# Expert rows by an indirect DMA from DRAM, and a scatter in two float32r passes

## The chip, the core and the metric

The kernel runs on one core of one Trainium2 chip. A core has a matrix engine (TensorE, PE, with its weight load PEld), VectorE (DVE), ScalarE (ACT), GpSimd (POOL) and SyncE (SP), and 16 DMA engines between DRAM and the on-chip memory. The metric is the device time of one execution in microseconds, as a median over runs.

## What is computed

Two transformer blocks over 512 tokens of 1024 features, in float32. The change lies in the last part of the first block, the expert choice: each of 16 experts takes the 64 tokens of highest affinity, applies its own gated network of three 1024 x 1024 matrices, and its results are added back to the rows of its tokens.

```python
def expert_choice_ffn(h, router_w, w_gate, w_up, w_down):
    cap = CAPACITY_FACTOR * n // N_EXPERTS                      # 64
    aff = jax.nn.softmax((h @ router_w).astype(jnp.float32), axis=-1)
    w_sel, idx = lax.top_k(aff.transpose(0, 2, 1), cap)
    xs = jax.vmap(lambda hb, ib: hb[ib])(h, idx)                # gather
    hid = jax.nn.silu(jnp.einsum('becd,edf->becf', xs, w_gate)) * jnp.einsum('becd,edf->becf', xs, w_up)
    ys = jnp.einsum('becf,efd->becd', hid, w_down) * w_sel[..., None]
    return ...zeros((n, d)).at[ib.reshape(-1)].add(yb.reshape(-1, d))   # scatter
```

Before it stand modulation, a gated linear recurrence, a convolution and an attention; after it the second block (pooling, delta rule, cross-attention with a memory, MLP).

## The kernel before

`build` (L1394 on) writes the program in stages. A scheduler orders each engine's instructions from the data dependences, the buffers of each tile and a priority by the order of the code, so the order of an engine need not be that of the source. Each engine works its list in order. Matrices of float32 are multiplied in two ways: as plain float32 (a matmul then shows as two records on PE), or split into a high and a low part of type float32r (`split`, L439: a cast on ACT, a subtraction on DVE), each product of parts being one record.

`route` (L796) computes the affinities `aff`, then the 64 largest of each expert by eight rounds of max and replace on DVE, and from them `slot`: for each token and expert its place among the 64, or a negative number. It also keeps `h2` (L834), the tokens times their 1/rms. While DVE does that, PE multiplies keys and values of the memory (`mem_kv`, eight units; L145 to L147 and L125 to L127); their results leave through `mst` (ACT) and a store on the GpSimd queue (`mk_dram`, `mv_dram`).

`expert_pair(p)` (L867) handles experts 2p and 2p+1 side by side, 64 rows each. `G` (L871) is a one-hot matrix of tokens by slots. `XT` is the pair's input, features by slots: 32 products of `h2` with `G` into PSUM (`xtp`, L880), then eight DVE operations with gain and shift (L883). Then come three products with the experts' matrices by `pair_mm` (L856): 32 matmuls each, alternating between the two halves of the PE columns, one half for each expert (L864, `pair`). After the gate product stand the sigmoid on ACT and DVE, `GT` (the transpose of `G`, through `gtp`) and `ws` (each slot's weight, through `wsp`, L899). After the up product the product of both is transposed (`htp`, L909) to `hT`, which shares its buffer with `XT` (L36, L907). After the down product DVE makes `ys`, the weighted rows (L915). `scatter` (L919) multiplies `GT` with `ys` for each tile of 128 tokens and half of the features (`sps`, L922, one plain float32 matmul), and DVE adds the result to the residual `x1` (L924). The program in front of the loop is short:

```python
        for p in range(8):
            last = self.expert_pair(p)
            if p == DL:
                self.delta_load()
            if p < 7:
                for t in range(4):
                    self.scatter(t, *last)
```

The last pair's scatter stands in `entry2` (L1006), which begins the second block. `delta_load` (L1034) brings constants of the second block on the GpSimd queue (`f2`, `maskf`, `baw`, `al`).

The weights come by `eload` (L845) on the SyncE queue: 24 loads of 1 MiB a pair, 192 in all. Two loads, one for each expert, serve eight matmuls, one step of `pair_mm`. They land in 18 buffers, nine for the even experts and nine for the odd ones, in fixed rotation; some are buffers that `mem_kv` used for its own weights. SyncE issues a load when PE has read its buffer for the last time. The first ten loads are issued ahead, beside the loads of the stages before.

Of the kernel before, what the change touches and what calls it, by code (L numbers as in the profile page):

```python
# [6 lines left out]
FT = mybir.dt.float32  # L7
FR = mybir.dt.float32r
U8 = mybir.dt.uint8
AF = mybir.ActivationFunctionType  # L10
# [4 lines left out]
D = 1024  # L15
KK = 8
S = 512
# [13 lines left out]
XB = 1  # L31
# [4 lines left out]
HT = lambda self: self.xtp  # L36
# [3 lines left out]
# columns of w_in  # L40
# [11 lines left out]
def shape_constants():  # L52
    i = np.arange(128)
    f = np.zeros((128, 466), np.float32)
# [11 lines left out]
    f[:, 450:466] = (np.float32(1.0) / np.arange(1, 17, dtype=np.float32))[None]  # L66
    f2 = np.zeros((128, 3, 128), np.float32)
# [11 lines left out]
class Net:  # L79
# [35 lines left out]
    def lin_f(self, *args, **kw):  # L115
        """ps[m, n] = W[:, c0:c0+m]^T X^T[:, t0:t0+n]"""
# [13 lines left out]
    def lin_f2(self, w, x, halves=False):  # L130
        """two tiles of lin_f; in halves of the tokens when the second half of x comes late"""
# [7 lines left out]
    def lin_n(self, ps, w, c0, x, t0, n, start=True, stop=True):  # L139
        """ps[128 tokens, n] = X[t0:t0+128] W[:, c0:c0+n]"""  # L140
# [11 lines left out]
    def rstd(self, ss, n, dst):  # L152
        """dst = (ss / n + eps) ** -0.5"""
# [4 lines left out]
    def log_sigmoid(self, dst, z, tmp):  # L158
        """dst = min(z, 0) - ln(1 + exp(-|z|)); tmp is overwritten"""
# [7 lines left out]
    def constants(self):  # L167
# [7 lines left out]
        self.kc = cp.tile([128, 466], FT, name="kc")  # L175
# [50 lines left out]
    def mod_cols(self, gs):  # L226
        """columns 256 g : 256 (g + 1) of the modulation, feature-major: four partial sums side by side, then their sum"""
# [18 lines left out]
    def pow_rstd(self, dst, ss, n, sub=None):  # L246
        """dst = (ss / n + eps) ** -0.5 for a few columns"""
# [4 lines left out]
    def norm_in(self):  # L252
        """self.hx: features by 512 latent tokens, self.hc: features by 256 context tokens, high and low parts"""
# [60 lines left out]
    def hgrn_head(self, hd, v):  # L314
        """both directions of a head. Index d: 0 forward, 1 backward, tokens in natural order, 256 context then 512 latent.
        F: products of the forget gates over blocks; Q[:, d]: keys times the gates from the key to the end of its block;
        R[:, 1 - d]: queries times the gates from the start of their block to the query. With blocks of m tokens, the pairs
        in neighbouring blocks of m come from the forward keys of the even blocks with the forward queries of the odd ones,
        and from the backward keys of the odd blocks with the backward queries of the even ones: one product for both."""
# [29 lines left out]
        # forget gate sigmoid(z), key sigmoid(-z)  # L349
# [9 lines left out]
        # products inside a chunk, transposed: the diagonal, then one level per block size  # L359
# [9 lines left out]
        def zigzag(x, n, m):  # L369
            """[n / 2m blocks, 2 halves, m]: the first row of x in the even blocks of m, its second row in the odd ones"""  # L370
# [3 lines left out]
        for lv in range(7):  # L374
# [10 lines left out]
            # blocks of twice the size  # L385
# [9 lines left out]
        # states: chunks 0, 1 are the context, 2 to 5 the latents  # L395
# [26 lines left out]
        # read-out: norm over the head, silu gate  # L422
# [27 lines left out]
    def gates(self, gate):  # L450
        """sigmoid(h W_gate)^T, a few products at a time, between those of others; self.sig holds it"""
# [13 lines left out]
    def merge(self, gate, wproj, first):  # L465
        """y^T (+)= sigmoid(h W_gate)^T * (o W_proj)^T, o in self.br"""
# [86 lines left out]
    def qk_stats(self, ps):  # L553
        """1 / rms of 2 token tiles of 4 heads of 64"""
# [8 lines left out]
    def qk_norm(self, dst, ps, stats, which, t):  # L563
        """dst[128, 2, 256] = 2 token tiles of 4 heads, normed, times the gain, rotated from tile t on"""
# [30 lines left out]
    def attn_keys(self, g):  # L595
        """[kh; kh] and [kl; kl] of a group of heads, 128 rows by 768 keys"""
# [993 lines left out]
```

## Time and profile before

| | us |
|---|---|
| device time, median of 3 runs (2608.29 to 2609.91) | 2608.99 |
| span of the profiled execution | 2604.0 |
| PE busy in it | 2528.8 (97%) |
| DVE, ACT busy | 1214.8, 982.5 |
| SyncE's queue, share of the 16 DMA engines over the span | 39.9% |

The profiled execution's own device time is not listed apart from its span; the runs are 5.0 us longer than the span. The rows further down are of five kinds. Windows give busy time, granted PE clock (1.00 is 2.4 GHz) and DMA rate of a stretch. The chain of waits follows what ended last backwards through the program and prints it in order of time, each piece with its start and length. The timeline lists instructions with the idle time ahead of them and what ended it. Groups by line give the busy time and the mean of one. DMA answers give the time from issue to landing. The expert stage runs from 1273 to 1790 us.

### The profile page before, as it was taken

To read this page: it belongs to the slowest core of one execution; us is meant where nothing else is said; L and a number is where in the kernel's file an instruction comes from. 1 tells how busy PE (TensorE), PEld (TensorE's weight loads), DVE (VectorE), ACT (ScalarE), POOL (GpSimd) and SP (SyncE) were. 2 spreads that over 40 slices of the span, in tenths; PEclk is the share of its full clock that TensorE was granted. 3 is DMA by queue.
4 is the path that set the end of the run, shared out by engine and by line. 5 is a ranking of instruction groups with operands and counts; after the bars stand their busy time and mean duration, and the time that the engine had idled before them with its cause. 6 is when DMAs were issued, how large, how long until landed. Compare 5 with 4: busy or idle time off the path is not lost.

```text
span 2604.0 us, 35253 instructions
## 1 busy us (share of the span) xinstructions
PE 2528.8 (97%) x14796; PEld 1927.7 (74%) x14796; DVE 1214.8 (47%) x1934; ACT 982.5 (38%) x1649; POOL 91.7 (4%) x116
## 2 busy tenths in 40 slices
PE   6999999999999999999999999998998999999998
PEld 4888888689887976679744444444778988889898
DVE  4558575734443565544422222124884464532433
ACT  4445445532234466633301000003665443431332
POOL 0000000000001110120100000000000010000000
PEclk9999999999999999999999999999999999999999
DMA  8223222422223210054899999994330032223331
GB/s 272 65 81 98 81 66 65 146 97 81 89 90 97 81 65 1 1 193 157 305 409 409 407 363 363 361 361 136 81 97 17 22 109 65 90 81 98 97 98 49
DMA packets 242494, 380.60 MB, mean 146 GB/s; under 512 B 6672, under 2 KB 188944, under 8 KB 242336
## 3 DMA queue, kind: packets, MB, share of 16 engines
q1 hardware_dynamic: 238784, 365.98, 39.9%
q0 software_dynamic: 3552, 12.38, 1.5%
q8 instruction: 116, 1.90, 0.3%
q14 instruction: 42, 0.34, 0.0%
HBM read 372.04 MB, written 4.19 MB: 144 GB/s over the span
## 4 chain that ended last, share of the span: by engine, by line
PE 80%; issue 12%; DVE 3%; ACT 3%; DMA 1%; POOL 0%; SPq 0%; POOLq 0%; ACTq 0%; DVEq 0%
PE pair L864 15%; PE lin L125 10%; PE lin L126 10%; PE lin L127 10%; PE lin L145 6%; PE lin L147 5%; PE lin L146 5%; PE xtp L880 2%; PE oT L717 2%; PE sps L922 2%; PE lps L383 2%; PE s L690 2%; PE ptp L704 1%; PE ups L408 1%; PE lin L234 1%
## 5 line engine op out<-in xcount | busy, mean ns | idle before, releaser
L112 DVE TENSOR_TENSOR wl<-raw,wh 128x1024 fp32r<-128x1024 f32 (+1 forms) x262 | 312.2, 1227 | 213.8 <-ACT wh L111 210.7
L111 ACT CAST wh<-raw 128x1024 fp32r<-128x1024 f32 (+1 forms) x262 | 258.4, 1028 | 400.1 <-PE lin L126 249.5
L864 PE MATMUL pair<-ew,XT 128*64 128x512 f32 x1024 | 239.4, 595 | 0.0
L127 PE MATMUL lin<-hx,wl 128*128 128x512 f32 x576 | 231.4, 402 | 0.0
L125 PE MATMUL lin<-hx,wh 128*128 128x512 f32 x576 | 229.8, 399 | 0.0
L126 PE MATMUL lin<-hx,wh 128*128 128x512 f32 x576 | 227.9, 396 | 0.0
L864 PEld LDWEIGHTS pair<-ew,XT 128*64 128x64 f32 x1024 | 81.9, 136 | 145.8 <-issue 139.9
L145 PE MATMUL lin<-wh,mh 128*128 128x256 f32 x512 | 145.0, 283 | 0.0
L147 PE MATMUL lin<-wh,ml 128*128 128x256 f32 x512 | 144.7, 283 | 0.0
L146 PE MATMUL lin<-wl,mh 128*128 128x256 f32 x512 | 144.0, 281 | 0.0
L864 PE MATMUL pair<-ew,hT 128*64 128x512 f32 x512 | 142.7, 599 | 0.0
L125 PE MATMUL lin<-hxh,wh 128*128 128x512 f32 (+1 forms) x352 | 131.6, 376 | 1.4 <-ACT hxh L941 1.3
L126 PE MATMUL lin<-hxl,wh 128*128 128x512 f32 (+1 forms) x352 | 131.8, 375 | 0.1
L127 PE MATMUL lin<-hxh,wl 128*128 128x512 f32 (+1 forms) x352 | 131.4, 374 | 0.0
L127 PEld LDWEIGHTS lin<-hx,wl 128*128 128x128 f32 x576 | 108.3, 188 | 25.7 <-issue 1.0
L125 PEld LDWEIGHTS lin<-hx,wh 128*128 128x128 f32 x576 | 108.4, 188 | 24.6 <-issue 1.2
L126 PEld LDWEIGHTS lin<-hx,wh 128*128 128x128 f32 x576 | 108.3, 188 | 24.7 <-issue 0.2
L864 PEld LDWEIGHTS pair<-ew,hT 128*64 128x64 f32 x512 | 44.7, 136 | 73.1 <-issue 68.7
L146 PEld LDWEIGHTS lin<-wl,mh 128*128 128x128 f32 x512 | 96.8, 189 | 0.1
L145 PEld LDWEIGHTS lin<-wh,mh 128*128 128x128 f32 x512 | 96.6, 189 | 0.1
L147 PEld LDWEIGHTS lin<-wh,ml 128*128 128x128 f32 x512 | 96.3, 188 | 0.0
L915 DVE SCALAR_TENSOR_TENSOR ys<-pair,ws,gfrow 128x512 f32<-128x512 f32 x16 | 12.0, 750 | 173.2 <-PE pair L864 172.3
(539 smaller groups left out, 5586.1 us busy)
## 6 DMA issues: line engine op xcount, KB each, us to landing
ew<-in_w_gate SPq DMA_DIRECT2D x64, 1024.0 KB, 14.1
ew<-in_w_up SPq DMA_DIRECT2D x64, 1024.0 KB, 14.2
ew<-in_w_down SPq DMA_DIRECT2D x64, 1024.0 KB, 8.7
raw<-in_w_in SPq DMA_DIRECT2D x34, 1024.0 KB, 5.1
raw<-in_w_in SPq DMA_DIRECT2D x52, 512.0 KB, 5.4
raw<-in_ada_w SPq DMA_DIRECT2D x24, 1024.0 KB, 6.3
raw<-in_w_up SPq DMA_DIRECT2D x16, 1024.0 KB, 5.6
raw<-in_w_down SPq DMA_DIRECT2D x16, 1024.0 KB, 5.2
```

The costliest lines, as they stand in the source:

```text
L111: nc.scalar.copy(wh[:, a:a + 4, :n], raw[:, a:a + 4, :n])
L112: nc.vector.tensor_sub(wl[:, a:a + 4, :n], raw[:, a:a + 4, :n], wh[:, a:a + 4, :n].bitcast(FT))
L125: self.nc.tensor.matmul(ps, a, xa, start=k == 0, stop=False)
L126: self.nc.tensor.matmul(ps, a, xb, start=False, stop=False)
L127: self.nc.tensor.matmul(ps, b, xa, start=False, stop=k == KK - 1)
L145: self.nc.tensor.matmul(ps, xa, a, start=start and k == 0, stop=False)
L146: self.nc.tensor.matmul(ps, xa, b, start=False, stop=False)
L147: self.nc.tensor.matmul(ps, xb, a, start=False, stop=stop and k == KK - 1)
L383: nc.tensor.matmul(ps[:, c].rearrange("p (b h x) -> p b h x", h=2, x=m), Xc[:, c], Y[:, c * n4:(c + 1) * n4], start=True, stop=True)
L690: nc.tensor.matmul(s[:, a:b], qT[2 * pair + hh][:, 128 * t:128 * t + 128], kT[p][:, a:b], start=p == 0, stop=p == 1)
L717: self.nc.tensor.matmul(self.oT[64 * hh:64 * hh + 64], self.vn[:, kt, 64 * g:64 * g + 64], PT[kt // 2][:, 2 * (kt % 2) + hh], start=kt == ...
L864: self.nc.tensor.matmul(ps[j][64 * e:64 * e + 64], lhs[:, k0 + k, 64 * e:64 * e + 64], w[e][:, k, 512 * j:512 * j + 512], start=k0 + k == ...
```

## The change

The normed tokens `h2` are no longer kept on chip: `route` writes them to a DRAM tensor `h2_dram` in four stores on the ScalarE queue, through two buffers. A table `affx` holds, for each token, the two affinities of a pair and the token's number (a new column of the constants). `expert_prep(p)` builds `G`, multiplies it with `affx` (`wsp`, three columns), casts the third column to an integer index `idx`, and starts an indirect DMA on GpSimd that brings the 128 token rows to `XG` (slots by features, one buffer). `expert_rows` transposes `XG` by eight PE transposes (`xtp`) and applies gain and shift as before. Pair 0 is prepared ahead of the loop; pair p+1 is prepared in `expert_pair(p)`, the gather written ahead of the up product, the transposes ahead of the down product. `hT` has its own buffer. `GT` becomes float32r, `ys` is split into high and low parts, and each scatter product is two float32r matmuls. Comments are also taken out, and line numbers shift.

```diff
@@ route
+        self.h2d = nc.dram_tensor("h2_dram", (S, D), FT, kind="Internal").ap()
+        for t in range(4):
+            h2 = rp.tile([128, D], FT, name="h2", bufs=2)
+            nc.scalar.activation(h2, x1[:, t], AF.Copy, scale=r[:, t:t + 1])
+            nc.scalar.dma_start(self.h2d[128 * t:128 * t + 128], h2)
...
-        self.h2 = sp.tile([128, 4, D], FT, name="h2")
-        for t in range(4):
-            nc.scalar.activation(self.h2[:, t], x1[:, t], AF.Copy, scale=r[:, t:t + 1])
+        self.affx = sp.tile([128, 4, 8, 3], FT, name="affx")
+        nc.vector.tensor_copy(self.affx[:, :, :, 0:2], aff.rearrange("p t (q e) -> p t q e", e=2))
+        nc.vector.tensor_copy(self.affx[:, :, :, 2:3], self.kc[:, 466:470, None, None].to_broadcast([128, 4, 8, 1]))
@@ expert_prep, expert_rows (new), expert_pair
-        XT = self.xtp.tile([128, KK, 128], FT, name="XT", bufs=XB)
+        ps = self.pp.tile([128, 3], FT, name="wsp", tag="tp", bufs=2)
+        for t in range(4):
+            nc.tensor.matmul(ps, Gf[:, t], self.affx[:, t, p], start=t == 0, stop=t == 3)
+        idx = self.sp.tile([128, 1], U32, name="idx", bufs=2)
+        nc.vector.tensor_copy(idx, ps[:, 2:3])
...
+        XG = self.xtp.tile([128, D], FT, name="XG", bufs=1)
+        nc.gpsimd.indirect_dma_start(out=XG, out_offset=None, in_=self.h2d,
+                                     in_offset=bass.IndirectOffsetOnAxis(ap=idx, axis=0), bounds_check=S - 1)
+        return Gf, ws, XG
...
+        XT = self.xtp.tile([128, KK, 128], FT, name="XT", bufs=1)
...
-                for t in range(4):
-                    nc.tensor.matmul(ps[:, j], self.h2[:, t, 128 * k:128 * k + 128], Gf[:, t], start=t == 0, stop=t == 3)
+                nc.tensor.transpose(ps[:, j], XG[:, 128 * k:128 * k + 128], self.ident)
...
-        GT = sp.tile([128, S], FT, name="GT", bufs=1)
+        GT = sp.tile([128, S], FR, name="GT", bufs=1)
...
+        if p < 7:
+            nGf, nws, XG = self.expert_prep(p + 1)
         u2 = self.pair_mm("w_up", p, XT)
-        hT = HT(self).tile([128, KK, 128], FT, name="hT", tag="XT", bufs=1)
+        hT = self.xtp.tile([128, KK, 128], FT, name="hT", bufs=1)
...
+        if p < 7:
+            self.pair = nGf, nws, self.expert_rows(XG)
         y2 = self.pair_mm("w_down", p, hT)
...
+            h, l = [sp.tile([128, 512], FR, name=f"ys{q}", bufs=2) for q in "hl"]
+            self.split(h, l, ys)
...
@@ scatter
-            self.nc.tensor.matmul(o, GT[:, 128 * t:128 * t + 128], ys2[j], start=True, stop=True)
+            for q in range(2):
+                self.nc.tensor.matmul(o, GT[:, 128 * t:128 * t + 128], ys2[j][q], start=q == 0, stop=q == 1)
@@ build
+        Gf, ws, XG = self.expert_prep(0)
+        self.pair = Gf, ws, self.expert_rows(XG)
         for p in range(8):
```

The scheduler's order on PE at the start of the stage, before (the last product of `mem_kv`, then pair 0):

```order
L147 MATMUL lin<-wh,mT_9130 128x256
L880 MATMUL xtp<-G,h_10124 128x128 x32
L864 MATMUL pair<-ew,XT 64x512 x32
L894 MATMUL gtp<-kc,G 128x128 x4
L899 MATMUL wsp<-aff,G 128x2 x4
L864 MATMUL pair<-ew,XT 64x512 x32
```

and after:

```order
L147 MATMUL lin<-wh,mT_9130 128x256
L884 MATMUL wsp<-affx,G 128x3 x4
L903 MATMUL xtp<-kc,XG 128x128 x8
L871 MATMUL pair<-ew,XT 64x512 x32
L923 MATMUL gtp<-kc,G 128x128 x4
L884 MATMUL wsp<-affx,G 128x3 x4
```

The 32 products ahead of the first gate product are gone; four short matmuls, the gather and eight transposes stand there.

On PE in the later pairs before, from the end of an up product to the scatter of the same pair (`hT` marks the down product, `XT` the next pair's gate):

```order
L909 MATMUL htp<-kc,sg 128x128 x8
L880 MATMUL xtp<-G,h_10124 128x128
L864 MATMUL pair<-ew,hT 64x512 x2
L880 MATMUL xtp<-G,h_10124 128x128 x6
L864 MATMUL pair<-ew,hT 64x512 x6
...
L864 MATMUL pair<-ew,hT 64x512 x14
L922 MATMUL sps<-ys,GT 128x512 x2
L864 MATMUL pair<-ew,XT 64x512
L922 MATMUL sps<-ys,GT 128x512 x2
```

and after:

```order
L934 MATMUL htp<-kc,sg 128x128 x8
L903 MATMUL xtp<-kc,XG 128x128 x4
L871 MATMUL pair<-ew,hT 64x512
...
L884 MATMUL wsp<-affx,G 128x3 x4
L871 MATMUL pair<-ew,hT 64x512 x24
L953 MATMUL sps<-ysh,GT 128x512
L871 MATMUL pair<-ew,XT 64x512
L953 MATMUL sps<-ysl,GT 128x512
L953 MATMUL sps<-ysh,GT 128x512
```

The one-hot products among the down product's matmuls are gone, and the `wsp` for the pair after the next stands there, so in the later pairs a gather is issued about a whole pair ahead of its transposes. The scatter still lies among the first matmuls of the next gate.

On GpSimd at the start of the stage before, with the waits of each instruction:

```order
L1001 DMA mv_dram<-mst 256x1x256 [waits DMASW7_49,Activation_49]
L1037 DMA f_11015<-in_kc 128x384 [waits DMASW5_49,DMASW6_49,DMASW4_49,DMASW7_49,DMASW2_49,DMASW0_49]
L209 DMA maskf<-in_km 128x448 [waits DMASW1_49,PE_49]
L1041 DMA baw<-in_w_in 128x8x8
L1043 DMA al<-in_ad 4x2 [waits DMASW3_49]
```

and after:

```order
L1032 DMA mv_dram<-mst 256x1x256 [waits DMASW7_49,Activation_49]
L1068 DMA f_11047<-in_kc 128x384 [waits DMASW5_49,DMASW6_49,DMASW4_49,DMASW7_49,DMASW2_49,DMASW0_49]
L891 DMA XG<-h_dram,idx 128x1024 [waits DMAHW4_49,DMAHW1_49,DMAHW5_49,DMASW1_49,DMAHW7_49,DVE_49,Pool_49]
L209 DMA maskf<-in_km 128x448 [waits PE_49]
L1072 DMA baw<-in_w_in 128x8x8 [waits DMASW3_49]
```

The first gather stands behind the load of `f2`, which waits for the landing of the stores ahead of it (`DMASW` are the semaphores of this queue's DMAs). The order of the weight loads on SyncE stays, but for two of the first up loads, which come behind a load of `mem_kv` instead of ahead of it.

## Rows read from the trace of the kernel before

**Rows 1.** Windows: busy us of PE, PEld, DVE, ACT, POOL; PEclk; DMA share; GB/s.

```profile
1290.00:1520.00 230.00, 228.79 (x1082) 100.41 (x1080) 49.04 (x90) 25.55 (x44) 0.56 (x1) 1.00 1.02 408
1530.00:1790.00 260.00, 258.86 (x1099) 107.86 (x1098) 53.82 (x104) 27.05 (x47) 0.00 (x0) 1.00 0.84 327
```

**Rows 2.** Chain of waits in an early pair: start us, us, what (x records).

```profile
1325.33 7.43 PE sps L922 x16
1332.76 6.92 PE xtp L880 x62
1339.68 13.88 PE pair L864 x64
...
1369.73 0.63 PE htp L909 x4
...
1384.66 7.43 PE sps L922 x16
```

**Rows 3.** Chain of waits in a late pair and at the stage's end.

```profile
1429.96 1.86 PE pair L864 x4
...
1433.36 3.58 PE pair L864 x12
...
1459.58 1.00 PE pair L864 x2
...
1476.72 20.76 PE pair L864 x92
...
1499.21 1.86 PE pair L864 x4
...
1775.98 13.95 PE pair L864 x64
...
1791.00 4.62 DMA fgrow<-in_rows
```

**Rows 4.** Timeline of PE in a projection with float32r parts.

```profile
302.47 0.39 PE L126 MATMUL lin<-hx,wh 128*128 128x512 f32 x1
302.70 0.39 PE L127 MATMUL lin<-hx,wl 128*128 128x512 f32 x1
```

**Rows 5.** Groups by line in 1270 to 1810: busy us, mean ns, idle before.

```profile
L924 DVE TENSOR_TENSOR x<-x,sps 128x512 f32<-128x512 f32 x64 | 43.5, 684 | 23.4 <-PE sps L922 23.2
...
L910 ACT COPY hT<-htp 128x512 f32<-128x512 f32 x16 | 9.4, 586 | 83.6 <-PE htp L909 83.6
```

**Rows 6.** SyncE's timeline at the start of the stage; landing of loads L853, 1100 to 1300.

```profile
1273.66 0.99 SPq L853 DMA_DIRECT2D ew<-in_w_down  x2
...
1283.96 0.88 SPq L853 DMA_DIRECT2D ew<-in_w_down  x2
...
DMA to landing us min/median/max: 4.9/8.4/15.9
```

**Rows 7.** Chain of waits at the start of the stage.

```profile
1273.21 7.14 PE xtp L880 x64
1280.35 13.88 PE pair L864 x64
```

**Rows 8.** GpSimd's timeline; DMA answers (KB, us to landing); weight loads issued 1270 to 1300.

```profile
1274.17 0.68 POOL L1001 DMA_DIRECT2D mv_dram<-mst  x1 [5.14 <-ACT mst L999]
1281.69 0.57 POOL L1037 DMA_DIRECT2D f<-in_kc  x1 [6.85 <-DMA mv_dram<-mst]
...
fgrow<-in_rows POOLq DMA_DIRECT2D x1, 512.0 KB, 4.6
...
mem<-in_mem POOLq DMA_DIRECT2D x1, 1024.0 KB, 10.5
...
DMA to landing us min/median/max: 5.7/11.4/15.9
```

**Rows 9.** Windows with PE partly idle, columns as in the first group.

```profile
20.00:30.00 10.00, 8.47 (x63) 2.91 (x56) 2.44 (x13) 1.18 (x4) 0.00 (x0) 1.00 1.04 333
1260.00:1265.00 5.00, 3.15 (x23) 2.93 (x22) 4.93 (x8) 0.52 (x2) 0.67 (x1) 0.85 0.72 251
```

More of the change, by code (lines that the diff above doesn't have):

```diff
@@ L9 @@
 U8 = mybir.dt.uint8
+U32 = mybir.dt.uint32
 AF = mybir.ActivationFunctionType
@@ L30 @@
 SOL = ((0, 8, 5, 1), (2, 9, 7, 3), (4, 6, 10, 11))
-XB = 1
 RB = 1
@@ L53, in shape_constants @@
     i = np.arange(128)
-    f = np.zeros((128, 466), np.float32)
+    f = np.zeros((128, 470), np.float32)
     f[:, :128] = np.eye(128)
@@ L66, in shape_constants @@
     f[:, 450:466] = (np.float32(1.0) / np.arange(1, 17, dtype=np.float32))[None]
+    f[:, 466:470] = i[:, None] + 128 * np.arange(4)[None]
     f2 = np.zeros((128, 3, 128), np.float32)
@@ L174, in constants @@
         nc.gpsimd.dma_start(self.pa, I["cols_a"])
-        self.kc = cp.tile([128, 466], FT, name="kc")
+        self.kc = cp.tile([128, 470], FT, name="kc")
         nc.gpsimd.dma_start(self.kc, I["kc"])
@@ L866, in pair_mm, with expert_prep @@
         return ps
-    def expert_pair(self, p):
-        nc, I, sp = self.nc, self.I, self.sp
+    def expert_prep(self, p):
+        nc = self.nc
         G = self.G[:, p % 2]
@@ L873, in expert_pair, with expert_rows @@
         Gf = G.rearrange("p t e s -> p t (e s)")
-        XT = self.xtp.tile([128, KK, 128], FT, name="XT", bufs=XB)
+        ps = self.pp.tile([128, 3], FT, name="wsp", tag="tp", bufs=2)
[3 more added lines that the diff above has]
+        nc.vector.tensor_copy(idx, ps[:, 2:3])
+        ws = self.sp.tile([128, 1], FT, name="ws", bufs=2)
+        for e in range(2):
+            nc.vector.tensor_copy(ws[64 * e:64 * e + 64], ps[64 * e:64 * e + 64, e:e + 1])
+        XG = self.xtp.tile([128, D], FT, name="XG", bufs=1)
+        nc.gpsimd.indirect_dma_start(out=XG, out_offset=None, in_=self.h2d,
+                                     in_offset=bass.IndirectOffsetOnAxis(ap=idx, axis=0), bounds_check=S - 1)
+        return Gf, ws, XG
+    def expert_rows(self, XG):
+        nc = self.nc
+        XT = self.xtp.tile([128, KK, 128], FT, name="XT", bufs=1)
         for a in range(2):
@@ L884, in expert_pair @@
                                         op0=OP.mult, op1=OP.add)
+        return XT
+    def expert_pair(self, p):
+        nc, I, sp = self.nc, self.I, self.sp
+        Gf, ws, XT = self.pair
         g2 = self.pair_mm("w_gate", p, XT)
@@ L894, in expert_pair @@
             nc.tensor.transpose(ps[:, 128 * t:128 * t + 128], Gf[:, t], self.ident)
-        GT = sp.tile([128, S], FT, name="GT", bufs=1)
+        GT = sp.tile([128, S], FR, name="GT", bufs=1)
         nc.scalar.copy(GT, ps)
-        ps = self.pp.tile([128, 2], FT, name="wsp", tag="tp", bufs=2)
-        for t in range(4):
-            nc.tensor.matmul(ps, Gf[:, t], self.aff[:, t, 2 * p:2 * p + 2], start=t == 0, stop=t == 3)
-        ws = sp.tile([128, 1], FT, name="ws", bufs=2)
-        for e in range(2):
-            nc.vector.tensor_copy(ws[64 * e:64 * e + 64], ps[64 * e:64 * e + 64, e:e + 1])
+        if p < 7:
+            nGf, nws, XG = self.expert_prep(p + 1)
         u2 = self.pair_mm("w_up", p, XT)
-        hT = HT(self).tile([128, KK, 128], FT, name="hT", tag="XT", bufs=1)
+        hT = self.xtp.tile([128, KK, 128], FT, name="hT", bufs=1)
         for j in range(2):
@@ L910, in expert_pair @@
             nc.scalar.copy(hT[:, 4 * j:4 * j + 4], ps)
+        if p < 7:
+            self.pair = nGf, nws, self.expert_rows(XG)
         y2 = self.pair_mm("w_down", p, hT)
-        ys2 = []
+        out = []
         for j in range(2):
@@ L915, in expert_pair @@
             nc.vector.scalar_tensor_tensor(ys, y2[j], ws, self.gfrow[:, 512 * j:512 * j + 512], op0=OP.mult, op1=OP.mult)
-            ys2.append(ys)
-        return GT, ys2
+            h, l = [sp.tile([128, 512], FR, name=f"ys{q}", bufs=2) for q in "hl"]
+            self.split(h, l, ys)
+            out.append((h, l))
+        return GT, out
     def scatter(self, t, GT, ys2):
```

1 line of the change is left out of this document (removed).

## The prediction

> **What bounds the kernel now.** The change touches the expert stage, so I looked for where that stage runs and which resource is short in it. The windows show it from 1273 to 1790 us with PE busy throughout, but with two different halves [rows 1]: in 1290 to 1520 the transfers run at 408 GB/s with the queues full (share 1.02), in 1530 to 1790 at 327 GB/s. So the weights press on the stage almost as hard as PE. A pair of experts needs 24 loads of 1 MiB, 25.17 MB, which at 0.408 MB/us take 61.7 us, or 2.57 us a load.
>
> The chain of waits gives PE's price for a pair. An early pair runs from one scatter to the next, 1325.33 to 1384.66: 59.3 us, less than the transfers need, so it eats from what was loaded ahead [rows 2]. A late pair, 1429.96 to 1499.21, takes 69.25 us, more than the transfers need [rows 3]: there PE is the bound, and SyncE waits for buffers. The reader should compare the pieces. Three products of 32 uninterrupted matmuls are 3 x 13.9 = 41.7 us in the early pair. In the late pair the scheduler has put the one-hot products and the scatter between them; its eleven runs of `pair` sum to 50.5 us (first 1.86 us for 4 records, last 20.76 us for 92). Two matmuls on the two column halves no longer run side by side at a run's end: 12 records alone take 3.58 us, where 12 x 0.217 = 2.6 would do. That is 8.8 us a pair for interruptions.
>
> **What the change removes on PE, per late pair.** (a) 32 one-hot products, 64 records, become 8 transposes. The records cost 6.92 us for 62 in one piece [rows 2] and 7.9 us plus two more records in pieces, 8.1 us in all; four transposes cost 0.63 us [rows 2], so eight 1.3. Gain 6.8 us. (b) The scatter: 8 fp32 matmuls cost 7.43 us [rows 2]. Two float32r passes are 16 matmuls of 128x512; the float32r projections follow each other at 0.23 us [rows 4], so 3.7 us. Gain 3.7 us. (c) Interruptions: the order of the changed kernel has runs of 1, 1, 6, 24, 1, 1, 3, 2 and 57 matmuls. By the rows of before, a run costs 0.43 us a matmul plus 0.57 where their number is odd (1.00 us for one) and 1.0 where it is even (1.86 for two, 20.76 for 46) [rows 3]: 41.3 + 6.4 = 47.7 instead of 50.5. Gain 2.8 us. (d) What it adds: the first scatter matmul now waits for the split of `ys` as well, a 0.6 us cast on ScalarE and a 0.7 us subtraction on VectorE (the sizes of the `hT` copy and of `x<-x,sps` addition) [rows 5]. Behind it on PE stand the next pair's gate matmuls, which have nothing to wait for but are in order. Between 0.6 (the subtraction hidden by the one gate matmul in between) and 2.6 (both halves in a row) us; I take 1.7. Net: 69.25 - 6.8 - 3.7 - 2.8 + 1.7 = **57.6 us** of PE per pair, in place of 59 to 69.
>
> **So the transfers become the bound.** 57.6 is less than 61.7. The gathers add to it: 128 rows of 4 KB, 0.52 MB, 1.3 us a pair by the same rate, 63.0 in all. From here I count the stage by the loads. There are 18 buffers for the loads. SyncE had issued the 18th by 1274.65, and the 19th only at 1283.96 [rows 6], when PE had finished the first step of the first gate: that product began at 1280.35 [rows 7], a step of 8 matmuls is 13.88 / 4 = 3.47 us, 1283.8. So the 19th load goes out 3.6 us after the gate product of pair 0 begins, and 174 loads remain. Everything depends on when that product begins.
>
> **The start, which gets worse.** Before, 32 one-hot products on PE (7.14 us) fill the time from 1273.2 to 1280.35 [rows 7]. After, PE sends the four `wsp` matmuls and then waits for the gather, which stands on GpSimd behind the load of `f2`. That load waits for the last `mv_dram` store: issued at 1274.17, and `f2` starts at 1281.69 after 6.85 us idle [rows 8]. The gather is therefore issued at about 1282.3. A delay on ScalarE comes ahead of it: `h2` is scaled through two buffers, so the third waits for a store, and the casts of the weights of `mem_kv` behind it wait too. Between 0 and 3 us of that reach PE (two scalings of 1.1 us and a store against one buffer of slack); I take 1.3, which moves the `mv_dram` store as well. The landing is not in the trace of before, since no indirect DMA is. The nearest rows are a 512 KB load on the same queue, 4.6 us, and a 1 MB one, 10.5 us [rows 8]; generating 128 addresses on GpSimd may cost more than a plain issue, so I take 6, with 4.6 and 10.5 as ends. The Trainium skill, "DMA: Bandwidth & Descriptors", section "Anatomy of one DMA", fits a GpSimd DMA by 2.0 us plus its bytes at 436 GB/s, an estimate of 3.2 us here; no run here shows that, the 4.6 us row is longer, and by the page the forecast would be 3 us lower. With 1282.3 + 1.3 + 6 = 1289.6, and 1.2 for four transposes and the first `XT` piece, the gate begins at **1291** (1288 to 1297) instead of 1280.35.
>
> PE then has been idle for some 16 us. After it had stood still for 1.85 of the 5 us from 1260 to 1265, the clock was granted at 0.85 on average there, so at 1.2 GHz for part of them [rows 9]. I let half of the first step run at 1.2 GHz: 3.47 + 1.7. The 19th load is issued at 1291 + 5.2 + 0.2 = 1296.5, 12.5 us later than before.
>
> **The sum.** 174 loads of 1.0486 MB and 7 gathers of 0.52 MB are 186.1 MB, at 0.408 MB/us 456 us. A lone load takes 4.9 us to land against 2.57 in the stream [rows 6], so 2.3 us on top: the last load lands at 1296.5 + 456 + 2.3 = 1754.8. The step on it is 3.5 us: PE ends the last product at **1758.3**, in place of 1775.98 + 13.95 = 1789.9 [rows 3]. PE by itself would be done at 1291 + 2 + 48 (pair 0, no scatter ahead) + 7 x 57.6 - 2 = 1742, so it has 16 us to spare, and every microsecond of (a) to (d) up to 2.3 a pair is hidden by the loads. At the end VectorE gets two more subtractions (1.4 us) ahead of the eight additions that it is busy with there, half hidden by the 4.62 us load of `fgrow` [rows 3]: +1. Gain 31.6 - 1 = 30.6 us. The profiled execution's span is 2604.0, 5.0 below the median of 2608.99, which I carry along: 2608.99 - 30.6 = **2578**. About 0.2% (5 us) is what a measurement of this kernel can tell from no change.
>
> **The rivals.** *The clock falls in the starved stretches* (7%). After the first pairs PE waits at each step, 3.47 us of work per 5.2 us of loads. For it: the dip above. Against: in 20 to 30 us PE was busy 8.47 of 10 us and stayed at full clock [rows 9]; and a step at 1.2 GHz takes 6.9 us, longer than its loads, so PE stops waiting. It can fall behind by one or two dips, 3 to 7 us, at the end: 2581 to 2585. In its extreme form (1%) each of the 96 steps runs at 1.2 GHz: 96 x 3.47 = 333 us on top of PE's own 1742, so some 2895, slower than before. The Trainium skill, "TensorE: Matmul & The Clock Gate", section "HAM oscillation", tells of a kernel that fell back to the low clock in every tile because it waited for its loads longer than it worked on them. The row of 20 to 30 us does not show that for waits like these.
>
> *PE stays the bound* (12%). If the scatter's waits or the interruptions are worse and a pair takes 62 us: 1291 + 50 + 7 x 62 - 2 = 1773, gain 16: 2593. For it: the scatter's additions on VectorE (0.68 us each for eight) pace PE through two PSUM buffers [rows 5].
>
> *The gathers come late: slower than before* (8%). `XG` has one buffer; the next gather is issued only when PE has read the last, and PE stands still at the transposes until it lands. With up to 18 weight loads outstanding, 46 us of transfers, a gather served after them would make pairs of gather plus some 5 us. From pair 0's start at 1291, the stage is slower than before from (1789 - 1341) / 7 = 64 us a pair, so from 59 us a gather; at 70 us: 1341 + 7 x 75 = 1866, 2685. For it: landings on that queue were measured with few loads outstanding. Against: the `mv_dram` store was done 7.5 us after its issue while the weight loads issued around it took 11.4 us in the median [rows 8], so that queue does not stand at the end of the line.
>
> *The weights come slower* (1%): the Trainium skill, "DMA: Bandwidth & Descriptors", section "Where 436 GB/s comes from", lets some 358 GB/s from HBM bind; 186.1 MB would take 520 us and the kernel would be slower by 33 us. The trace does not agree: 408 GB/s for 230 us.
>
> *It gives all of it back* (3%): a start at 1310 or later and pairs near 61 us, within 5 us of before. *A better start* (6%): gather landed by 1285 with the clock up, and smaller waits: below 2566.
>
> **How the numbers follow.** The forecast has 62%, with 2568 to 2588 (landing 4.6 to 10.5 us, ScalarE delay 0 to 3, gathers at one to one and a half times their bytes). Faster: 62 + 7 + 12 + 6 = 87%; same 3%; slower 8 + 1 + 1 = 10%. The range reaches up to PE as the bound and down to a good start: 2563 to 2598.
>
> **What would show it.** After: the transfers at about 408 GB/s through the whole stage, without the fall to 327 [rows 1]; PE idle for 12 to 20 us at the start of the stage with GpSimd's gather as the releaser, then short waits for `ew` instead of none; SyncE waiting less for `pair`; last `pair` near 1758. Wrong would be: PE without waits for `ew` (then PE is the bound), waits for `XG` in every pair, or a low clock over more than some 10 us.

## The result and the profile after

The changed kernel takes 2580.91 us (median; 2578.95 to 2581.14), the kernel before beside it 2609.45 (2608.29 to 2612.09): ratio 0.9892, 95% interval 0.9879 to 0.9905, 28.5 us less. The profiled execution's span is 2577.1 us against 2604.0.

Windows of the changed kernel; columns as in [rows 1]: length, busy us of PE, PEld, DVE, ACT and POOL, granted PE clock, DMA share, GB/s.

```profile
1277.70:1294.80 17.10, 5.68 (x18) 2.80 (x20) 2.64 (x8) 0.20 (x1) 5.47 (x8) 0.50 0.62 229
1296.50:1757.50 461.00, 441.28 (x1831) 162.85 (x1827) 114.35 (x218) 60.23 (x102) 7.74 (x8) 1.00 1.02 407
1530.00:1760.00 230.00, 215.25 (x842) 77.95 (x839) 50.16 (x94) 29.66 (x51) 2.60 (x3) 1.00 1.02 406
1764.00:1790.00 26.00, 17.47 (x61) 12.70 (x62) 21.30 (x45) 15.72 (x32) 5.71 (x7) 0.54 0.47 151
```

The second half of the stage, at 327 GB/s and PE without a pause before [rows 1], now runs at 406 GB/s, and PE is idle for 6% of it. Instead, the start has a stretch with PE at 1.2 GHz (0.50), after it stood still for the gather, and the transfers at 229 GB/s. Behind the stage PE is at 1.2 GHz for most of 26 us (0.54).

GpSimd's timeline of the changed kernel: start us, us, what, idle time before and its releaser.

```profile
1274.06 0.67 POOL L1032 DMA_DIRECT2D mv_dram<-mst  x1 [5.25 <-ACT mst L1030]
1281.63 0.57 POOL L1068 DMA_DIRECT2D f<-in_kc  x1 [6.91 <-DMA mv_dram<-mst]
1282.72 1.13 POOL L891 DMA_INDIRECT XG<-h_dram,idx  x1 [0.51 <-DMA ew<-in_w_down]
...
1723.52 0.59 POOL L1063 DMA_DIRECT2D fgrow<-in_rows  x1 [97.04 <-PE pair L871]
```

The first two rows are those of [rows 8], at the same times; the gather stands behind them. The 0.51 us ahead of it stand in other runs of the same order with the label `issue`, so they are not that load's. The chain of waits goes on from there, and ends in the last step of the last pair (start us, us, what):

```profile
1282.72 6.36 DMA XG<-h_dram,idx
1289.12 1.97 PE xtp L903 x8
1291.09 9.30 PE pair L871 x33
...
1738.61 18.84 DMA ew<-in_w_down
1757.50 3.66 PE pair L871 x12
```

The gate product of pair 0 begins at 1291.1 instead of 1280.35 [rows 7], the last `pair` product ends at 1761.2 instead of 1789.9 [rows 3]. PE is now kept waiting by loads of weights; the most common of these waits is that of its weight loads (PEld) for `w_up`, 28.2 us in 32 places, the longest 2.8. PE itself overlaps part of them and stands idle for 19 us of 1300 to 1757:

```profile
PEld pair L871 <- DMA ew<-in_w_up: 28.2, 32, 2.8
```

SyncE's timeline shows the 19th load, which went out at 1283.96 before [rows 6]:

```profile
1296.56 3.80 SPq L860 DMA_DIRECT2D ew<-in_w_down  x3
```

Its waits for `pair` in 1300 to 1760 are half of what they were in 1300 to 1790 before (323.4 us in 130 places):

```profile
SPq L860 <- PE pair L871: 164.2, 84, 5.3
```

### The profile page after: what moved, and what is told of

Its sections match the earlier page's. It is cut to its first block, busy times and chain, and to the rows that moved or that the text cites. A ratio compares the mean times of both kernels' runs of the same rounds, so it can differ in the third digit from the quotient of the medians.

```text
span 2577.1 us, 34426 instructions
## 1 busy us (share of the span) xinstructions
PE 2468.7 (96%) x14348; PEld 1877.8 (73%) x14348; DVE 1225.0 (48%) x1960; ACT 992.7 (39%) x1665; POOL 99.9 (4%) x124
## 4 chain that ended last, share of the span: by engine, by line
PE 83%; DMA 7%; DVE 5%; ACT 4%; issue 1%; POOL 0%; SPq 0%; POOLq 0%; ACTq 0%; DVEq 0%
PE lin L125 11%; PE lin L126 11%; PE lin L127 11%; PE pair L871 10%; PE lin L145 6%; PE lin L147 6%; PE lin L146 6%; DMA ew<-in_w_up 4%; PE oT L717 2%; PE lps L383 2%; DMA ew<-in_w_down 2%; PE s L690 2%; PE ptp L704 1%; PE sps L953 1%; PE dyp L1235 1%
## 5 line engine op out<-in xcount | busy, mean ns | idle before, releaser
L871 PE MATMUL pair<-ew,XT 128*64 128x512 f32 x1024 | 259.1, 602 | 11.1 <-DMA ew<-in_w_up 11.1
L871 PE MATMUL pair<-ew,hT 128*64 128x512 f32 x512 | 135.3, 598 | 1.8 <-DMA ew<-in_w_down 1.8
L145 PE MATMUL lin<-wh,hx 128*128 128x256 f32 x320 | 91.1, 285 | 0.4 <-DVE sig L499 0.4
## 6 DMA issues: line engine op xcount, KB each, us to landing
ew<-in_w_gate SPq DMA_DIRECT2D x64, 1024.0 KB, 18.9
ew<-in_w_up SPq DMA_DIRECT2D x64, 1024.0 KB, 18.5
```

The source lines that it names most:

```text
L145: self.nc.tensor.matmul(ps, xa, a, start=start and k == 0, stop=False)
L871: self.nc.tensor.matmul(ps[j][64 * e:64 * e + 64], lhs[:, k0 + k, 64 * e:64 * e + 64], w[e][:, k, 512 * j:512 * j + 512], start=k0 + k == ...
```

## The experiments

A time without an interval is a median; ratios are to runs of the kernel before on the same chip. "Tail" is the time from the end of the last `pair` product to the first `lin` of the second block (before 1789.9 to 1814.7, 24.8 us; after 25.8).

**The change without its second part.** In `expert_pair` and `scatter` (`GT` is float32 again as well):

```
-            h, l = [sp.tile([128, 512], FR, name=f"ys{q}", bufs=2) for q in "hl"]
-            self.split(h, l, ys)
-            out.append((h, l))
+            out.append(ys)
...
-            for q in range(2):
-                self.nc.tensor.matmul(o, GT[...], ys2[j][q], start=q == 0, stop=q == 1)
+            self.nc.tensor.matmul(o, GT[...], ys2[j], start=True, stop=True)
```

> The change with its second part undone: rows by gather, scatter as one fp32 matmul per tile and column half, no split. Theory (weight transfers bound the stage): PE's work per pair goes up by the scatter's 3.7 us and down by the shorter wait, and stays below the 63 us that 24 loads and a gather take, so nothing of it shows: the last pair product ends within 2 us of 1761, and the time is 2577 to 2584 us against 2581 for the whole change; the split at the end falls away (about 1 us). Rival (PE is the bound after the change): 8 x 3.7 = 30 us longer less the missing waits, 2595 to 2610.

Measured: 2572.5 us, ratio 0.9864 (0.985 to 0.9878). The window is as full of transfers as with the two passes:

```profile
1530.00:1750.00 220.00, 209.33 (x810) 74.32 (x808) 47.55 (x88) 23.78 (x41) 2.59 (x3) 1.00 1.03 409
```

The last product ends at 1757.6, 3.5 us earlier than in the change, where the theory allowed 2; 2.5 of it is the start (its gather landed in 4.37 us instead of 6.36). So the pairs take the same time with either scatter, within 1 us over the stage, and PE is not the bound. But the time is 8 us below the change, below what the theory allowed: the tail is 22.6 us instead of 25.8. The experiments on the tail follow that up.

**The second part alone**, on the kernel before (one weight buffer of 18 given up for room): the same lines with the other sign, and

```
-            p, b = (...)[(0, 0, 0, 0, 1, 1, 2, 2, 3)[self.neven % 9]]
+            p, b = (...)[(0, 0, 0, 0, 1, 1, 2, 2)[self.neven % 8]]
```

> The kernel before with the second part alone: rows by one-hot products from the chip's own copy, scatter as two float32r passes over split values; one of the 18 weight buffers (ewx) is given up to make room, which costs at most one load, 2.6 us. Theory: the late pairs are bound by PE at 69 us, so here the scatter's 3.7 us less its added wait of 1.7 show in the pairs that PE bounds, some 5 of 8: about 10 us, less 2.6: 2597 to 2605, so that most of the change's 28.5 us belongs to the gather. Rival (both parts matter alike): half of the 28.5, 2595 or below. If the order of PE's work gets worse with more pieces between the pair products, 2609 to 2625.

Measured: 2605.9 us, ratio 0.9988 (0.998 to 0.9997): 3 us, less than either expectation. Chain of waits, one pair apart:

```profile
1461.69 0.75 DVE ys L915
...
1529.71 0.75 DVE ys L915
```

A late pair takes 68.0 us instead of 69.25, so the second part gains 1.25 us of PE's time a pair, not 2. Some of it is lost again: pair 1, whose order changed too and which has a buffer less, takes 66 us instead of 59, and the split lies in the tail; the last product ends only 2.2 us earlier (1787.8). The change's gain belongs to its first part, the rows by gather with their transposes and `hT`'s own buffer, which alone has the ratio 0.9864 above; these three were not taken apart.

**The first gather early.** `G`, `idx`, `ws` and `XG` go into the pool `mop`, and

```
         self.ahead = [("w_up", 0, k0) for k0 in (0, 2, 4, 6)] + [("w_gate", 1, 2)]
+        self.G = self.mop.tile([128, 2, 4, 2, 64], FT, name="G")
+        Gf, ws, XG = self.expert_prep(0)
         self.mem_kv(range(MU, 8))
...
-        Gf, ws, XG = self.expert_prep(0)
         self.pair = Gf, ws, self.expert_rows(XG)
```

> The change with the first gather moved ahead of the second part of mem_kv (its buffer, its index and the one-hot tile live in an earlier pool), so that it no longer stands on GpSimd behind the load of f2, which waits for the last mv_dram store. Theory (the start counts one to one, since every later load follows from it): the first gate product begins at 1275 to 1277 instead of 1291.1, without the idle time its first step runs at full clock, and the last pair product ends 15 to 19 us earlier, at 1742 to 1746: 2562 to 2566 us. Rival (PE or the buffers bound the late pairs, and the start is slack): under 5 us, 2576 to 2581.

Measured: 2570.0 us, ratio 0.9854 (0.984 to 0.9868). The edit moves the whole preparation of pair 0 ahead of half of `mem_kv`, so that GpSimd issues the gather 16 us earlier, and the last product ends at 1746.97 + 3.65 = 1750.6:

```profile
1266.81 1.14 POOL L891 DMA_INDIRECT XG<-h_dram,idx  x1 [4.31 <-DVE ws L889]
...
1746.97 3.65 PE L871 MATMUL pair<-ew,hT 128*64 128x512 f32 x12 [0.66 <-DMA ew<-in_w_down]
```

The gate begins at 1275.4, 15.6 us earlier, at full clock, but the stage ends only 10.5 us earlier, less than the theory's 15 to 19 and more than the rival's 5. The windows tell why. First the changed kernel, then the early gather:

```profile
1220.00:1300.00 80.00, 62.93 (x474) 55.92 (x475) 36.72 (x74) 21.95 (x34) 10.29 (x15) 0.87 0.73 254
```

```profile
1220.00:1300.00 80.00, 77.46 (x567) 61.01 (x568) 40.76 (x83) 27.56 (x44) 11.39 (x16) 1.00 0.84 308
```

54 GB/s more for 80 us are 4.3 MB, 10.6 us at 409 GB/s. Not the time of the first product counts, but the transfer time that was left unused. With the early gather the DMA engines have hardly any left from 1260 on (386 to 398 GB/s in 1260 to 1290, share 1.01 to 1.03), so the rest of the 15.6 us is hidden.

**Four of 24 loads a pair left out** (the second expert's `w_down`, pairs 1 to 7: its result is another):

```
-            w = [self.eload(src, 2 * p + e, k0) for e in range(2)]
+            w = [self.eload(src, 2 * p + e, k0) for e in range(1 if src == "w_down" and p else 2)]
+            if len(w) == 1:
+                w = w + w
```

> The change with four of the 24 loads of each pair but the first left out: in the product with w_down both experts use the rows of the first one (so the second expert's result is another). PE's work is the same. Theory (transfers bind at 63 us a pair): with 20 loads and a gather they need 52.7 us, and PE becomes the bound at its own pace. By the prediction's 57.6 us a pair the last product ends at 1742 to 1746 and the time is 2562 to 2567; if PE's pace is nearer to the 54 to 55 us that the first pairs of the changed kernel took, it ends near 1727 and the time is 2545 to 2550. Rival (PE is the bound already): no change, 2577 to 2584.

Measured: 2525.9 us, ratio 0.9684 (0.9668 to 0.97). With the same work on PE the kernel is 55 us faster, so the loads were the bound. Chain of waits, one pair apart:

```profile
1495.24 0.76 DVE ys L944
...
1548.67 0.76 DVE ys L944
```

PE by itself takes 53.4 us a pair (the order here has fewer pieces), 4 less than the prediction's 57.6. My expectation was too high at both values.

**The gathers' bytes** (pairs 1 to 7 use the rows of pair 0), **beside the change itself**:

```
+        if p == 0:
+            self.XG = ...  # the gather, once
-        return Gf, ws, XG
+        return Gf, ws, self.XG
```

> The change with the first gather alone: pairs 1 to 7 use the rows of pair 0 (other results), everything else is as in the change. Theory (the stage is bound by the bytes that come in, the gathers' too): 7 x 0.524 MB at 0.409 MB/us are 9.0 us, the last pair product ends 8 to 10 us earlier than in the change and the time is lower by as much. Rival (gathers come on a queue of their own and cost the weight stream nothing): within 1.5 us of the change. Rival (each gather costs more than its bytes): over 12 us lower.

> The changed kernel itself, beside the others on the same chip, so that 2572.5 us for the fp32 scatter can be read against it. Theory (the float32r scatter costs time at the end of the stage): 2577 to 2583 us, and the first lin of the second block 25 to 26 us behind the last pair product, against 22.6 with the fp32 scatter. Rival (the 8 us between them were the spread between chips and runs): 2571 to 2575.

Measured: the change again 2578.9 us, ratio 0.9889 (0.9874 to 0.9904); with one gather 2570.7, 0.9857 (0.9842 to 0.9872). The last step of the last product begins here (with one gather; in the change again at 1757.00):

```profile
1748.71 3.65 PE L871 MATMUL pair<-ew,hT 128*64 128x512 f32 x12 [0.66 <-DMA ew<-in_w_down]
```

8.3 us, and 8.2 in the medians, for 9.0 us of bytes. The gathers cost the stage their bytes, and no more. That the change again is 2578.9 also shows that the 2572.5 of the fp32 scatter was not the spread between chips and runs.

**The tail: fp32 for the last pair alone.**

```
+            if p == 7:
+                out.append((ys,))
+                continue
             h, l = [sp.tile([128, 512], FR, name=f"ys{q}", bufs=2) for q in "hl"]
```

> The change with the last pair's scatter alone as fp32, without a split; pairs 0 to 6 keep the two float32r passes. Theory (the split is hidden by the transfers in seven pairs and costs only behind the last one, where the two subtractions, the wait for them and the clock that fell are all on the path): all of the fp32 scatter's gain comes back, 4 to 6 us below the change in the same comparison, and the first lin of the second block 22 to 23.5 us behind the last pair product instead of 25.8. Rival (the fp32 scatter gains in the pairs): within 1.5 us of the change.

Measured: 2573.0 us, ratio 0.987 (0.9855 to 0.9885), 5.8 below the change in the same comparison; tail 22.6 us against 25.2. So the two passes gain nothing in seven pairs and cost in the last. In the profiles, whose spans differ by 7.1, the tail is 2.6 of the difference and the start, whose gather lands sooner or later in any kernel, 1.7. Another 1.6 lies in the second block, between the transposes `bgc` and the product `gr` (14.2 us against 12.6), where PE's granted clock was 0.78 in 1820 to 1825 of the change again and 1.00 here; the changed kernel's first profile has 12.6 too, so that is not the scatter's. The rest I could not place.

**Does the clock do it?** In the change PE ran at 1.2 GHz over most of the tail, as the window above shows. Two kernels give PE extra work there that nobody reads: 16 more float32r passes in the last scatter,

```
+            if warm:
+                z = self.pp.tile([128, 512], FT, name="warm", tag="tp", bufs=2)
+                for q in range(2):
+                    self.nc.tensor.matmul(z, GT[...], ys2[j][q], start=q == 0, stop=q == 1)
```

> The change with 16 more float32r passes on PE in the last pair's scatter, of the same operands into a tile that nobody reads, so that PE works there about as long as with fp32 matmuls; the split stays. Theory (the split itself costs the 1 to 1.5 us that its cast and subtractions take, and the rest of the 5 us behind the last product comes from the clock, which falls because the faster passes leave PE idler): the clock stays at full level until the transposes of the entry, the first lin of the second block begins 23.5 to 24.5 us behind the last pair product instead of 25.2 to 25.8, and the time is 2 to 4 us below the change: 2574 to 2577. Rival (the split's work on VectorE is all of it): 25 us or more, 2578 to 2582.

and with them five fp32 matmuls on `xf[2]` and `xf[3]`:

> The 16 extra float32r passes in the last scatter, and five fp32 matmuls more on the scaled rows of token tiles 2 and 3, which fill PE's 5 us between the last scatter and the first transpose of the entry (in the run without them the clock fell just there, 1.2 GHz from 1775 to 1790 us). Nobody reads their result; the split stays. Theory (of the 5 us behind the last product some 1 to 1.5 are the split's work, the rest is the low clock under the transposes and the first lin): the clock stays up, the first lin begins 23.3 to 24.3 us behind the last pair product instead of 25.2 to 26.1, the bgc transposes 55 to 56.5 us behind it instead of 57.6 to 60.6, and the time is 2575 to 2578 us. Rival (VectorE paces the entry whatever the clock): lin at 25 us or later, 2579 to 2582.

Measured: 2580.8 us and 2575.4 us (0.9887, 0.9872 to 0.9902; 0.9871, 0.9855 to 0.9888). Windows of the first, then of the second:

```profile
1764.00:1790.00 26.00, 17.43 (x73) 14.21 (x74) 20.72 (x44) 15.72 (x32) 5.71 (x7) 0.70 0.46 150
1775.00:1790.00 15.00, 10.65 (x47) 9.64 (x48) 10.67 (x28) 7.79 (x18) 3.81 (x4) 0.50 0.18 64
```

```profile
1764.00:1790.00 26.00, 20.00 (x112) 14.75 (x111) 19.76 (x43) 15.44 (x32) 5.71 (x7) 1.00 0.44 145
```

In the first the low clock only comes later, and the tail is 26.1. In the second PE stays at 2.4 GHz throughout and the tail is still 24.75, where the theory said 23.3 to 24.3. So up to the first `lin` the clock is worth 0.4 to 1.3 us (the change has 25.2 and 25.8 in its two profiles), not 3 to 4: the theory fell, though the second kernel's time lies in its range. Its third sign missed as well: the `bgc` transposes came 57.2 us behind the last product.

The low clock also costs time behind the tail. From the first `lin` to `bgc` nine of the profiles take 32.4 to 32.5 us, all with PE at 1.00 there; the other five take 33.6 to 34.6, with a granted clock of 0.96 to 0.93, among them the change (33.6) and the first of these two kernels (34.5). Of the 4.3 us between the spans of the two kernels, 0.8 lie ahead of the last product's end, 1.3 in the tail and 2.0 in this stretch. Between the second kernel and the change again the spans differ by 1.3 only, the medians by 3.5; the rest of that I could not place.

**What it is instead.** GpSimd's timeline at the norm of the entry, for the change again, for fp32 in the last pair, and for fp32 in the last pair with the early gather:

```profile
1774.89 1.04 POOL L1057 TENSOR_TENSOR ss<-ss,mhalf 128x4 f32<-128x4 f32 x1 [1.14 <-DVE ss L1056]
...
1778.08 1.03 POOL L1057 TENSOR_TENSOR ss<-ss,mhalf 128x4 f32<-128x4 f32 x1 [1.24 <-DVE ss L1056]
```

```profile
1772.14 2.54 POOL L1060 TENSOR_TENSOR ss<-ss,mhalf 128x4 f32<-128x4 f32 x2
```

```profile
1766.87 1.04 POOL L1060 TENSOR_TENSOR ss<-ss,mhalf 128x4 f32<-128x4 f32 x1 [1.13 <-DVE ss L1059]
...
1770.06 1.03 POOL L1060 TENSOR_TENSOR ss<-ss,mhalf 128x4 f32<-128x4 f32 x1 [1.24 <-DVE ss L1059]
```

These are the two power operations, of token tiles 0 and 1 and of 2 and 3. Counted from the end of the last product (1760.6, 1758.7, 1753.9), the second begins at 17.4, at about 15.0 (it ends at 16.0), and at 16.1. In the change's first profile it begins at 17.1, and with the early gather and the split at 16.9. In the first and third the second waits for `ss` on VectorE, which stands there behind the scaling `nx` of tiles 0 and 1 (1.42 us); in the second kernel the order puts both powers side by side. So of 2.4 us the split's own work is 1.3 (0.8 by the profile with 16.9), about what its two subtractions take (0.68 us each), and the order that the scheduler found for it 1.1. That the order differs is seen; that it would cost as much alone was not tried. The kernel before has the slower order too, with fp32.

**Both costs taken off.** The early gather with fp32 in all pairs, the same with a 19th weight buffer (`ewx` with two), and the early gather with fp32 in the last pair alone:

> The first gather moved ahead of the second part of mem_kv, and the scatter as one fp32 matmul for all pairs. Theory (two separate costs, the gap in the transfers at the start, 10.5 us, and the split at the end, 4 to 5 us): both come off, last pair product at 1748 to 1751, 2562 to 2567 us, below the 2570 of the early gather alone. Rival (the order of PE's work with fp32 pieces bounds the pairs once the start is earlier): 2569 to 2575.

> The first gather early, all scatters fp32, and the room that the split values leave used for a second buffer of weights in the pool ewx, 19 instead of 18. Theory (the stage ends when the last byte has come, and one more load ahead of the stage is one less in it): 2.6 us below the same kernel with 18 buffers, last pair product at 1747 to 1749, 2562 to 2565 us. Rival (before the stage the transfers have no free time for it, 353 GB/s of 409 at 1240 to 1250): within 1 us of it, 2565 to 2567.

> The first gather early, the two float32r passes in pairs 0 to 6, and fp32 for the last pair's scatter alone. Theory (the float32r passes are hidden by the transfers in the seven pairs, also with the earlier start): as with fp32 in all pairs, 2564 to 2568 us, last pair product at 1749 to 1752. Rival (PE's shorter pairs count once the start is earlier): 2560 or below.

Measured: 2566.1 us (0.9837, 0.9824 to 0.985), 2566.3 (0.9832, 0.9819 to 0.9845) and 2570.9 (0.9849, 0.9835 to 0.9862). The first adds up as forecast and beats both kernels, the changed one by 13 us in the same comparison (2578.9). The 19th buffer brings nothing, as the rival said: up to 1300 no more has come in than with 18. The same windows, with 18 and with 19 buffers:

```profile
1220.00:1300.00 80.00, 76.99 (x566) 60.65 (x566) 40.74 (x83) 27.40 (x44) 11.37 (x16) 1.00 0.84 310
```

```profile
1220.00:1300.00 80.00, 76.97 (x564) 60.77 (x566) 40.76 (x83) 27.55 (x44) 11.37 (x16) 1.00 0.84 307
```

The third missed its range: its tail is 23.9, with the order of the powers shown above; from the first `lin` to `bgc` it takes 34.4 us where the first takes 32.5, at a clock of 0.94; its stage ended 3 us later (2.6 of it were there already at the power of `route`, ahead of all that was changed), and the two passes in seven pairs gain nothing with the earlier start either.

## Why the prediction was right, step by step

**The bound.** Transfers at 409 GB/s from 1300 to the last load, as forecast, and they hold for the changed kernel in three experiments: less to load is faster (four loads a pair, seven gathers), more work on PE is not slower. A late pair of the change shows it (chain of waits):

```profile
1592.81 18.83 DMA ew<-in_w_up
...
1611.68 3.66 PE pair L871 x12
...
1636.28 0.74 DVE ys L942
...
1647.38 7.88 PE pair L871 x35
...
1655.49 18.85 DMA ew<-in_w_up
```

62.7 us from load to load; the forecast said 63.0.

**PE's price for a pair** was put at 57.6 us; where PE waits for no load the change takes 55.5, between this `ys` and the next:

```profile
1392.91 0.76 DVE ys L942
...
1393.70 0.63 ACT ysh L440
...
1394.37 0.49 PE sps L953
1394.86 1.00 PE pair L871 x2
1395.86 0.89 PE sps L953 x3
...
1398.88 1.86 PE pair L871 x6
...
1401.87 1.01 PE pair L871 x4
...
1404.02 25.05 PE pair L871 x114
...
1448.41 0.76 DVE ys L942
```

(a) The transposes cost 1.0 us instead of 1.3. (b) The 16 passes cost 4.8 us, not 3.7: each piece between others begins with a slow one (0.49 us; four take 1.12 to 1.14). (c) The runs of `pair` sum to 45.2 us, not 47.7. The rule that I took from [rows 3], by odd and even numbers, was wrong. What runs side by side is the second expert's matmul and the first expert's that follows it, a unit of 0.87 to 1.01 us. A run that begins with the first expert's spends a unit on it alone: two matmuls from the start of a product take two units (1.86 in [rows 3]), three take two as well (x6 records, 1.86), but two that begin with the second expert's take one (x4 records, 1.01). The count of matmuls since the product's start gives this for each run in both kernels. (d) From the last matmul that `ys` needs to the first pass it is 1.5 us, 1392.89 to 1394.37 (1.7 forecast). The second part alone confirms (b) and (d): 7.4 - 4.8 - 1.5 = 1.1 us a pair, 1.25 measured. None of this reached the time, since the pairs are bound by 63 us. The prediction said that too: up to 2.3 us a pair are hidden.

**The start** came as forecast: gather behind `f2`, issue at 1283.6 (measured 1282.72), landing 6 us (6.36), gate at 1291 (1291.1), 19th load at 1296.5 (1296.56). Half of the first step at 1.2 GHz was right too: the granted clock was 0.50 to 1294.8 and 1.00 from there, and the gate product took 1.86 us longer than the 13.88 of [rows 7] (1.7 forecast):

```profile
1291.09 15.74 PE pair L871 x64
```

Two details differ and cancel, which is luck: the 1.3 us for ScalarE did not reach GpSimd (1274.06 against 1274.17), and the landing and the transposes ahead of the gate, at 1.2 GHz, took 8.3 us instead of 7.2. The Trainium skill, "DMA: Bandwidth & Descriptors", section "Anatomy of one DMA", has a fit that gives 3.2 us for the landing, an estimate; the first gathers took 4.4 to 8.2 us in the runs here, so the row of a 512 KB load was the better guide.

**The sum.** The last load landed at 1757.45, not 1754.8, the last product ended at 1761.2, not 1758.3. The rate was a little better (409 for 408, 1 us), but 187.4 MB came in, not 186.1 (3 us): `fgrow` (0.52 MB), which the program now fetches within the stage, the second block's first loads (0.44 MB), which share the engines with the last experts' loads, and code (0.3 MB). That is the term that was mis-sized. Of the 28.8 us that the last product ends earlier, the spans keep 26.9; the medians differ by 28.5.

**The tail** was put at +1 us, and is +1.0 in the profiled execution (24.8 to 25.8), but not by the terms forecast; that the size fits is luck. VectorE's wait for `fgrow` before, and the second power (before, then after):

```profile
1795.70 1.22 DVE L1016 TENSOR_TENSOR xf<-x,fgrow 128x1024 f32<-128x1024 f32 x1 [0.86 <-DMA fgrow<-in_rows]
...
1806.99 1.04 POOL L1026 TENSOR_TENSOR ss<-ss,mhalf 128x4 f32<-128x4 f32 x1 [1.24 <-DVE ss L1025]
```

```profile
1778.25 1.03 POOL L1057 TENSOR_TENSOR ss<-ss,mhalf 128x4 f32<-128x4 f32 x1 [1.24 <-DVE ss L1056]
```

The load of `fgrow`, 4.62 us long [rows 3], held VectorE up for 0.86 us. That wait is gone, since GpSimd issues the load at 1723.5, and the split's own work, 0.8 to 1.3 us, stands in its place: the second power begins 17.1 us behind the last product in both kernels. The +1.0 lies behind it, 8.7 us to the first `lin` instead of 7.7, with PE at 1.2 GHz. The forecast had no such term, and none for the 1.1 us that the low clock costs up to `bgc` (33.6 against 32.5).

**A sign of being wrong** did show, a low clock over more than some 10 us: 17 us around the gather, while PE mostly stood still, and some 24 behind the last product. Neither lies where the loads bind; the first cost what was forecast, the second the two microseconds above.

**The rivals.** *The clock falls*: in the changed kernel it stayed at 1.00 from 1300 to 1760, though PE waited for loads by up to 1.9 us at a time. The Trainium skill, "TensorE: Matmul & The Clock Gate", section "HAM oscillation", describes a kernel that fell back at each wait for loads; this stage does not show it, with PE busy for 94% of the time. In the change again, and in three more kernels, the clock fell once in the stage: there PE waited 2.0 us for `w_up`, and the clock was 0.75 in 1550 to 1555. It cost nothing that shows: the transfers stayed at 409 GB/s, and the last product ended at 1760.7. The prediction's argument against this rival misread [rows 9], though: the trace of before has no record of the clock until 31.3 us, so the 1.00 printed for 20 to 30 us is not measured, and the same 16 matmul records took nearly twice as long there as just after (start us, us, what):

```profile
27.88 1.94 PE L234 MATMUL lin<-raw,cst 128*32 128x256 f32 x16
31.73 1.07 PE L234 MATMUL lin<-raw,cst 128*32 128x256 f32 x16
```

So PE was at 1.2 GHz there, and the row is no evidence against the rival; that the stage kept its clock is. *PE stays the bound*: refuted by the fp32 scatter, which adds to PE's pairs (56.5 us where they wait for no load) and lengthens nothing. *Gathers late*: PE waited for `XG` once, for pair 0. The gathers landed in 6.4 to 8.6 us, the weight loads in 18.5 to 18.9 (the medians of the three matrices), so the gathers don't queue behind them; the Trainium skill, "DMA: Bandwidth & Descriptors", section "Queues, rings and completion order", says that each DMA engine takes its queues in turn, and the trace agrees. *Weights at 358 GB/s*: 409 were measured, with one core running.

## What to carry to other kernels

Once a stage's transfers run without a pause, cost an edit by what it does to the bytes and to the stretches in which the transfers stand still; work taken off an engine that keeps the transfers' pace was worth nothing here, and its price showed where the stage ends. Look for what a new DMA stands behind, on its queue and in the program: here the first gather's index was there at 1274.1, but the gather stood behind a load that had nothing to do with it until 1282.7. Preparing pair 0 earlier, ahead of that load and of half of `mem_kv`, was worth 10 us, more than a third of the whole change; moving the gather past the load alone was not tried. Count every byte in the stretch, also the next stage's first loads and the small tables.

## What the runs showed of the hardware that I had not expected

- An indirect DMA of 128 rows of 4 KB holds GpSimd for 1.0 to 1.1 us and lands 7.4 to 9.0 us after its issue while 409 GB/s of other loads are under way (the first ones, with fewer loads beside them, 4.4 to 6.4); it takes no more of the transfer rate than its bytes (1.2 us a gather by the run with one of them, 1.28 by its bytes).
- Of fp32 matmuls on alternating column halves, the one on the second half runs beside the next one on the first half, not the other way round: a run of two takes 1.01 us or 1.86, by the half that it begins with, and a single one 1.00. Where a run is cut costs up to 0.9 us.
- A float32r pass of 512 columns follows another at 0.23 us, but the first one after other work takes 0.49, so 16 passes in five pieces cost 4.8 us instead of 3.7.
